# A second level of Strassen's algorithm for one of the seven gate and up products, and the down weights' sums moved to VectorE

## The chip, the cores and the metric

The kernel runs on one core of one Trainium2 chip. The metric is the device time of one execution in microseconds (us), the median over the runs shown; the profile is one further execution, recorded instruction by instruction.

## The reference

One layer of a hybrid encoder on 2048 tokens of width 1024: a combined projection, forgetting attention beside a multi-scale pooling, attention to 256 memory tokens, and a gated feed-forward. Each part adds to the residual stream h. The change lies in the last part:

```python
D_FF = 2816
hn = rmsnorm(h, g_ffn[l])
gu = jnp.einsum('bsd,df->bsf', hn, w_gate_up[l])        # 2048 x 1024 times 1024 x 5632
act = jax.nn.silu(gu[..., :D_FF]) * gu[..., D_FF:]
h = h + jnp.einsum('bsf,fd->bsd', act, w_down[l])       # 2048 x 2816 times 2816 x 1024
```

All of it is fp32.

## The kernel before

**Words and products.** A matmul here takes fp32r operands, which keep only part of an fp32 number. So each operand is split in two words: ACT casts it to the high word, VectorE subtracts that from the original to get the low word (`sub_hi`, L64; the cast is on L1137 for gate and up weights, L184 for `split`). `mm3` (L66 to L71) forms a product of two such pairs with three matmuls: high times high (L69), high times low (L70), low times high (L71). With a contraction of 128 a chunk, a product over 512 of the width is 4 chunks, 12 matmuls.

**Feed-forward, gate and up** (`gate_up`, from L1518). The tokens are handled in two passes (`ps_`) of 1024. The 2816 features are 22 tiles `t` of 128. For one tile the weights are a 2 x 2 block matrix: two halves of the width of 1024 (512 each) by gate and up (128 features each), b11, b12, b21, b22; the pass's tokens are x11, x12, x21, x22: two groups of 512 tokens by the two halves of the width. One level of Strassen's algorithm (Winograd's form) makes the four results from seven products instead of eight: b11 with x11, b21 with x12, t4 with x22, b22 with s4, t2 with s2, t1 with s1, t3 with s3, where t1 to t4 are sums of weight blocks and s1 to s4 sums of token blocks. Each product is 12 matmuls of 512 columns, 84 a tile. `product` (L1513) issues one; `weight_steps` (L1130) makes the weights' words and sums (splits on L64, sums on L1140).

PSUM has eight banks of 512 fp32 columns. A tile uses a, b and c, banks 0 to 2 or 3 to 5 in turn. a collects b11, then t2, then t3 on top of each other, and after each step ACT copies the running sum to SBUF (s1 on L1534, s2 on L1566, s3 on L1572); t4 of this tile follows in the next tile's turn. b holds t1, later b22 on top. c holds b21 with x12, and VectorE adds it to s1 (L1551), after which ACT applies silu (L1552): that is the first token group's gate. The order on TensorE for tile t, with the tile before it interleaved, is: b11, t4 of t-1, b21, b22 of t-1, t2, t1, t3. Banks 6 and 7 are free for the late token tiles of the first pass.

**What is ready when.** The token operands' words of a pass are kept in SBUF: four of them in large slabs (`SLABS`: x11, x12, s2, s1; they appear in the trace under the slabs' old names qs, kh, kl, cb) and three made at the start of the stage (`late_ops`: s3, x22, s4) from raw tiles `xr`, loaded from DRAM. Weight words go to eight places ww0 to ww7 in turn (`word_pair`), seven parts a tile. The raw weights of a tile (`graw`, 1 MB) have two buffers. `temp` (L1438) hands out [128, 512] fp32 tiles from a pool of 14: the copies s1, s2, s3, the activations and their sums, raw operands.

**Side jobs in the first pass** are hung on places in the tile loop (`early`, L1670 on): (t, n) is a place in tile t. From tile 4 on, the last four token tiles are normalised and turned (`late_tile`; PE transposes to banks 6 and 7, VectorE multiplies them into `hst`). For each pair of tiles, `load_down` brings a 1 MB group of down weights (`wdr`), and `down_sums` (L1482) makes their four Strassen sums on POOL (L1486) and stores them to DRAM for the down product, which both passes read. POOL also makes the activations' sums (`act_sums`, L1510).

**Feed-forward, down** (`down`): per pass seven products over 11 pairs of feature tiles, each step with one split of activations and one of weights; in the first pass's down, the second pass's token operands are made in between (`next_ops`).

**Order of the work.** In this stage TensorE and SP (the queue that issues the loads) run in the order in which the code is written (`in_order(EN.SP)`). For ACT, VectorE and POOL a planner fixes the order beforehand from modelled costs and due times; each engine then works through its queue in that order, and waits where an input is missing. A tile of a pool is taken by whichever instruction is next in the planner's time when one is free.

Of the kernel before, what the change touches and what calls it, by code (L numbers as in the profile page):

```python
# [16 lines left out]
P = 128  # L17
S = 2048
D = 1024
KD = D // P  # L20
# [21 lines left out]
def block_kernel(ctx: ExitStack, tc: tile.TileContext, x, xT, memT, cols, rows, w_qkvf, w_p, w_pool, w_out,  # L42
# [1013 lines left out]
    SLABS = ("x11", "x12", "s2", "s1")  # L1056
# [6 lines left out]
    late_d = {op: [dr.tile([P, FT], F32, name=f"{op}d{j}") for j in range(4)] for op in ("s3", "s4")}  # L1063
# [66 lines left out]
    def weight_steps(raw, w, tie=()):  # L1130
        b = {(kh, a): raw[:, 4 * kh:4 * kh + 4, a] for kh in range(2) for a in range(2)}
        quad = lambda v: v.rearrange("p (k c) -> p k c", k=4)
        sum_ = lambda n: quad(hp.tile([P, FT], F32, tag="cm", name=n, bufs=3)[:])

        def put(nm, v):
            w[nm] = hi, lo = word_pair()
            needs(act.copy(quad(hi), v), *(tie if nm == "t2" else ()))  # L1137
            sub_hi(quad(lo), v, quad(hi))

        sub = lambda o, p_, q_: dve.tensor_tensor(out=o, in0=p_, in1=q_, op=ALU.subtract)  # L1140
# [12 lines left out]
        put("t3", b[0, 1])  # L1153
        sub(b[1, 0], b[1, 0], t2)
        put("t4", b[1, 0])
        put("b22", b[1, 1])
        yield

    def weight_ops(raw, tie=()):
        w = {}  # L1160
        for _ in weight_steps(raw, w, tie):
            pass
        return w
# [270 lines left out]
    with hps, ExitStack() as c0:  # L1434
# [3 lines left out]
        temp = lambda n: fb.tile([P, FT], F32, tag="t", name=n, bufs=14)[:]  # L1438
        bank = lambda n: fps.tile([P, FT], F32, tag=f"bk{n}", name=f"bk{n}", bufs=1)[:]
        OPS = ("x11", "x12", "s2", "s1", "s3", "s4", "x22")  # L1440

        def late_ops():

            for op in ("s4", "s3", "x22"):
                ops[op] = [tuple(fb.tile([P, FT], F32R, tag=f"{op}{c}{j}", name=f"{op}{c}{j}", bufs=1)[:]
                                 for c in "hl") for j in range(4)]

        def load_late(op):

            late_raw[op] = [temp("xr") for _ in range(4)]  # L1450
            for j in range(4):
                sp.dma_start(late_raw[op][j], hTd[1][j + 4] if op == "x22" else late_d[op][j][:])
# [3 lines left out]
        def put_late(op):  # L1456
            for j in range(4):
                hi, lo = ops[op][j]
                needs(act.copy(hi, late_raw[op][j]), *(emptied[:1] if op in ("x22", "s3") else ()))
                sub_hi(lo, late_raw[op][j], hi)  # L1460

        late_raw = {}

        def late_tile(i):
# [3 lines left out]
            for a, hv in enumerate(halves):  # L1468
                sp.dma_start(hv, h2d[i][:, a * FT:(a + 1) * FT])
                act.activation(bank(6 + a), hv, AF.Square, scale=1.0 / 32.0, accum_out=ms[:, a:a + 1])  # L1470
# [5 lines left out]
            def turn_(a):  # L1476
                turn_normed(i, 4 * a, halves[a], bank(6 + a).rearrange("p (k t) -> p k t", k=4),
                            fb.tile([P, 4, P], F32, tag="hst", name="hst", bufs=1))
# [3 lines left out]
        def down_sums(k):  # L1482

            raw = down_raw.pop(k)
            b11, b12, b21, b22 = (raw[:, n] for n in range(4))
            sub = lambda o, p_, q_: pool.tensor_tensor(out=o, in0=p_, in1=q_, op=ALU.subtract)  # L1486
# [5 lines left out]
            for nm, v in (("t3", t3), ("t1", b12), ("t2", b22), ("t4", b21)):  # L1492
                pool.dma_start(wsum[k][nm][:], v)
# [3 lines left out]
        def load_down(k):  # L1497
            down_raw[k] = raw = wdp.tile([P, 4, FT], F32, tag="wd", name="wdr", bufs=1)
            for c in range(2):
                sp.dma_start(raw[:, 2 * c:2 * c + 2],  # L1500
                             w_down[:, (2 * k + c) * P:(2 * k + c + 1) * P, :].rearrange("a p c -> p a c"))
# [15 lines left out]

        def gate_up(ps_, between, follow, head, turned=0):  # L1518

            prev = None  # L1520
            blocks = {}
            for t in range(NF + 1):
                cur = None
                if t < NF:
                    for job in between.get((t, 0), ()):
                        job()
                    w = head if t == 0 and head else weight_ops(weights_raw(t, hp, "v"), copied[4:5] if t == 5 else ())
                    for job in between.get((t, 1), ()):
                        job()
# [3 lines left out]
                    s1 = temp("s1")  # L1533
                    emptied.append(act.copy(s1, a))  # L1534
                    for job in between.get((t, 2), ()):
                        job()
                else:
                    next(follow)
                if prev:
                    k, odd = divmod(prev["t"], 2)  # L1540
# [4 lines left out]
                    blocks["a22" if odd else "a21"] = prev["s3"]  # L1545
                    pool.dma_start(actd[prev["t"]][2 * ps_ + 1][:], prev["s3"])
                    if odd:
                        act_sums(ps_, k, blocks, ("s1", "s2"))
                if cur:
                    product(c, w["b21"], "x12", True)  # L1550
                    dve.tensor_tensor(out=s1, in0=c, in1=s1, op=ALU.add)  # L1551
                    act.activation(s1, s1, AF.Silu)  # L1552
                    cur["s1"] = s1
                else:
                    next(follow)
                if prev:
                    product(prev["b"], prev["w"]["b22"], "s4", False)
                    dve.tensor_tensor(out=prev["s2"], in0=prev["b"], in1=prev["s2"], op=ALU.add)
                    dve.tensor_tensor(out=prev["s2"], in0=prev["s2"], in1=prev["s1"], op=ALU.mult)
                    blocks["a12" if odd else "a11"] = prev["s2"]  # L1560
                    pool.dma_start(actd[prev["t"]][2 * ps_][:], prev["s2"])
                    act_sums(ps_, k, blocks, ("s4",) if odd else ("s3",))
                if cur:
                    product(a, w["t2"], "s2", False)
                    cur["s2"] = temp("s2")
                    copied.append(act.copy(cur["s2"], a))  # L1566
                    for job in between.get((t, 3), ()):
                        job()
                    product(b, w["t1"], "s1", True)
# [95 lines left out]
        with in_order(EN.SP):  # L1665
            for op in ("s3", "x22", "s4"):
                load_late(op)
            late_ops()
            turns = {}
            early = {(0, 2): [lambda: put_late("s3")], (0, 3): [lambda: put_late("x22")], (1, 1): [lambda: put_late("s4")]}  # L1670
# [4 lines left out]
            early.setdefault((0, 1), []).append(lambda: load_down(0))  # L1675
            for k in range(NK - 1):
                if k:
                    early.setdefault((2 * k + 2, 1), []).append(lambda k=k: load_down(k))
# [10 lines left out]

            for ps_ in range(2):  # L1690
# [53 lines left out]
```

## Time and profile before

| | us |
|---|---|
| median of 3 runs | 2486.38 (2486.14 to 2488.24) |
| the profiled execution | 2486.17 |
| its span, first to last instruction | 2484.4 |
| gate and up, first pass | about 1220 to 1637 of the span |
| down, first pass | about 1637 to 1848 |
| gate and up, second pass | about 1848 to 2268 |
| down, second pass | about 2268 to the end |

The granted TensorE clock was 0.999 of full speed on average. PE is TensorE's matmuls, PEld its weight loads, DVE is VectorE, ACT ScalarE, POOL GpSimd. A row of a group reads: line, engine, operation, tiles out<-in, shapes, count | busy us, mean ns of one | idle time of the engine just before, and what ended it. A row of a timeline reads: start, length, engine, line, operation.

### The profile page before, as it was taken

Reading aid. Unit: us, or ns where it says so; the run is one execution under the profiler, and the core shown is the slowest. Engines: PE = TensorE matmul, PEld = TensorE weight load, DVE = VectorE, ACT = ScalarE, POOL = GpSimd, SP = SyncE. Lnnn points to the kernel's source line nnn. Section 1 sums busy time; section 2 is a strip of 40 time slices with the busy share of each in tenths; the row PEclk is TensorE's granted clock in tenths of the full one; section 3 lists DMA queues with packets and bytes.
Section 4 is the critical chain, followed back from the end, with each engine's and each line's share of the span. In section 5 each row is a group of like instructions: output and inputs, shape, how many; then the busy total and the mean of one; then the engine's idle time right before and its main releaser. Section 6 shows DMA issues by size and latency. Waiting matters only on the chain.

```text
span 2484.4 us, 36567 instructions
## 1 busy us (share of the span) xinstructions
PE 2468.4 (99%) x12899; PEld 2109.2 (85%) x12899; DVE 1662.4 (67%) x3000; ACT 1204.0 (48%) x2308; POOL 745.1 (30%) x1012
## 2 busy tenths in 40 slices
PE   9999999999999899999999999999999999999999
PEld 8999989878888788888888888888888888888887
DVE  7444495489999855556868787667676666665554
ACT  6434341089999835445633433335443333333443
POOL 2223200045556524343135545430002222222000
PEclk9999999999999999999999999999999999999999
DMA  8665566476776443233645544467762333325666
GB/s 295 216 191 173 163 210 180 150 197 159 177 166 156 120 149 112 106 111 134 233 158 182 193 174 167 172 230 251 259 239 98 106 119 115 107 98 198 229 204 212
DMA packets 218279, 428.95 MB, mean 173 GB/s; under 512 B 25952, under 2 KB 101728, under 8 KB 207264
## 3 DMA queue, kind: packets, MB, share of 16 engines
q1 hardware_dynamic: 187920, 330.12, 42.4%
q0 software_dynamic: 30032, 96.23, 10.4%
q8 instruction: 102, 1.67, 0.3%
q14 instruction: 81, 0.66, 0.1%
q10 hardware_dynamic: 144, 0.26, 0.0%
HBM read 287.47 MB, written 134.61 MB: 170 GB/s over the span
## 4 chain that ended last, share of the span: by engine, by line
PE 83%; DVE 1%; issue 1%; POOL 1%; ACT 0%; DVEq 0%; POOLq 0%; ACTq 0%
PE bk L71 17%; PE bk L69 17%; PE bk L70 17%; PE acc L917 5%; PE sps L841 5%; PE tp L56 4%; PE mmps L69 4%; PE mmps L71 4%; PE mmps L70 4%; PE oo L69 1%; PE oo L70 1%; PE oo L71 1%; PE zp L71 1%; PE zp L69 1%; PE zp L70 1%
## 5 line engine op out<-in xcount | busy, mean ns | idle before, releaser
L64 DVE TENSOR_TENSOR ww<-draw,ww 128x512 fp32r<-128x512 f32 x308 | 209.7, 719 | 151.1 <-ACT ww L184 150.6
L184 ACT CAST ww<-draw 128x512 fp32r<-128x512 f32 x308 | 179.2, 620 | 220.9 <-PE bk L71 175.3
L64 DVE TENSOR_TENSOR ww<-graw,ww 128x512 fp32r<-128x512 f32 x220 | 174.3, 798 | 107.8 <-ACT ww L1137 107.6
L70 PE MATMUL bk<-ww,ww 128*128 128x512 f32 x619 | 240.2, 388 | 0.0
L71 PE MATMUL bk<-ww,ww 128*128 128x512 f32 x619 | 240.2, 388 | 0.0
L69 PE MATMUL bk<-ww,ww 128*128 128x512 f32 x619 | 240.1, 388 | 0.0
L1137 ACT CAST ww<-graw 128x512 fp32r<-128x512 f32 x220 | 136.0, 622 | 179.5 <-PE bk L71 164.4
L64 DVE TENSOR_TENSOR pl<-tp,ph 128x512 fp32r<-128x512 f32 (+3 forms) x298 | 177.5, 598 | 7.3 <-ACT ph L950 6.6
L69 PE MATMUL zps<-wh,xhi 128*128 128x384 f32 (+1 forms) x512 | 174.1, 340 | 0.0
L71 PE MATMUL zps<-wh,xl 128*128 128x384 f32 (+1 forms) x512 | 172.0, 336 | 0.0
L70 PE MATMUL zps<-wl,xhi 128*128 128x384 f32 (+1 forms) x512 | 171.9, 336 | 0.0
L950 ACT CAST ph<-tp 128x512 fp32r<-128x512 f32 (+3 forms) x298 | 152.7, 529 | 24.3 <-PE tp L56 22.9
L69 PE MATMUL bk<-qs,ww 128*128 128x512 f32 x352 | 137.8, 391 | 0.0
L71 PE MATMUL bk<-qs,ww 128*128 128x512 f32 x352 | 137.2, 390 | 0.1
L70 PE MATMUL bk<-kh,ww 128*128 128x512 f32 x352 | 136.9, 389 | 0.0
L69 PE MATMUL bk<-kl,ww 128*128 128x512 f32 x352 | 136.9, 389 | 0.0
L70 PE MATMUL bk<-cb,ww 128*128 128x512 f32 x352 | 136.9, 389 | 0.0
L71 PE MATMUL bk<-kl,ww 128*128 128x512 f32 x352 | 136.9, 389 | 0.0
L71 PEld LDWEIGHTS bk<-ww,ww 128*128 128x128 f32 x619 | 116.2, 188 | 24.1
L70 PEld LDWEIGHTS bk<-ww,ww 128*128 128x128 f32 x619 | 116.2, 188 | 24.0
L69 PEld LDWEIGHTS bk<-ww,ww 128*128 128x128 f32 x619 | 116.2, 188 | 23.7
L1615 POOL DMA_DIRECT2D out_dram<-o x31 | 16.7, 541 | 374.9 <-DVE o L1612 373.0
(641 smaller groups left out, 7066.1 us busy)
## 6 DMA issues: line engine op xcount, KB each, us to landing
graw<-in_w_gu_dram SPq DMA_DIRECT2D x44, 1024.0 KB, 5.6
draw<-in_w_down_dram SPq DMA_DIRECT2D x66, 256.0 KB, 4.4
xl<-in_xT_dram SPq DMA_DIRECT2D x64, 256.0 KB, 5.5
wdr<-in_w_down_dram SPq DMA_DIRECT2D x22, 512.0 KB, 4.3
xrow<-in_x_dram SPq DMA_DIRECT2D x16, 512.0 KB, 4.8
vd<-cb SPq DMA_DIRECT2D x16, 512.0 KB, 3.6
kh<-qkT1h SPq DMA_DIRECT2D x16, 512.0 KB, 10.3
kl<-qkT1l SPq DMA_DIRECT2D x16, 512.0 KB, 12.3
```

The lines of the kernel that those rows point to most:

```text
L56: return pe.transpose(out.bitcast(F32R), src, identr[:])
L64: (eng or dve).tensor_tensor(out=lo, in0=src, in1=f(hi), op=ALU.subtract)
L69: pe.matmul(ps, lhsT=sh, rhs=mh, start=first, stop=False, skip_group_check=goes_on)
L70: pe.matmul(ps, lhsT=sh, rhs=ml, start=False, stop=False, skip_group_check=goes_on)
L71: pe.matmul(ps, lhsT=sl, rhs=mh, start=False, stop=last, skip_group_check=goes_on)
L184: act.copy(hi, raw)
L841: pe.matmul(ps[:, :w], lhsT=qs[:, i * P:(i + 1) * P], rhs=kk[:, cs], start=(a == 0), stop=(a == 1))
L917: pe.matmul(acc[:m, q0 * P:], lhsT=v[:, j, :m], rhs=(pl if low else ph)[:, q0 * P:], start=state["n"] == 1, stop=state["n"] == 2 * nk)
L950: act.copy(ph[:, sl], tp[:, sl])
L1137: needs(act.copy(quad(hi), v), *(tie if nm == "t2" else ()))
L1615: pool.dma_start(out[rows_, cs], o)
```

## The change

**Weights and products.** The product b21 with x12, two of which belong to a pair of feature tiles (even t, odd t+1), is made for the pair at once: the two tiles' b21 side by side are 512 of the width by 256 features, x12 is 512 of the width by 512 tokens. Both are cut in 2 x 2 blocks (256 of the width by 128 features; 256 of the width by 256 tokens), and the same form of Strassen's algorithm gives seven quarter products, each of 2 chunks, that is 6 matmuls of 256 columns. The odd tile's turn issues all seven, between the other products; the order there is b11, three quarters, t4 of t-1, two quarters, b22 of t-1, two quarters, t2, t1, t3. In even tiles the order is b11, t4 of t-1, b22 of t-1, t2, t1, t3. In tile 0, where there is no tile before, t1 comes ahead of t2: b11, t1, t2, t3. The quarters gather in halves of bank 7 (u) and of the c banks, and VectorE adds them to s1 of both tiles in six sums of 256 columns and one of 512; both silus follow at the end of the odd tile's quarters.

```diff
@@ weight_steps
         put("b11", b[0, 0])
-        put("b21", b[1, 0])
...
+        if pair is None:
+            t4 = b[1, 0]
+            sub(t4, b[1, 0], t2)
+        else:
+            t4 = b[0, 0]
+            sub(t4, b[1, 0], t2)
+            odd = b[1, 0]
+            put_half(pair, "h11", "h21")
+            both = sum_("ht")
+            sub(both[:, :2], odd[:, :2], pair[:, :2])
+            sub(both[:, 2:], odd[:, 2:], both[:, :2])
+            put_half(both, "ht1", "ht2")
+            sub(odd[:, :2], odd[:, 2:], odd[:, :2])
+            put_half(odd, "ht3", "h22")
+            sub(pair[:, 2:], pair[:, 2:], both[:, 2:])
+            put_half(pair[:, 2:], "ht4")
@@ gate_up
+                        if odd:
+                            pair = fb.tile([P, 4, P], F32, tag="pair", name="pair", bufs=1)[:]
+                            sp.dma_start(pair, w_gu[t - 1].rearrange("p (k a c) -> p k a c", k=KD, a=2)[:, 4:, 0])
...
+                if odd:
+                    u, c0, c1 = bank(7)[:, :B], bank(3 * ((t + 1 + turned) % 2) + 2), c[:, B:]
+                    s0 = prev["s1"]
+                    quarter(u, w["h11"], "a11", True)
+                    quarter(c1, w["ht1"], "s1", True)
+                    quarter(c0[:, :B], w["h21"], "a12", True)
+                    add(s0[:, :B], u)
+                    add(s1[:, B:], c1)
...
-                if cur:
-                    product(c, w["b21"], "x12", True)
-                    dve.tensor_tensor(out=s1, in0=c, in1=s1, op=ALU.add)
-                    act.activation(s1, s1, AF.Silu)
...
+                if odd:
+                    quarter(u, w["ht2"], "s2", False)
+                    quarter(c1, w["h22"], "s4", False)
+                    add(s1[:, :B], u)
+                    add(s1[:, :B], c1)
...
+                if odd:
+                    quarter(u, w["ht3"], "s3", False)
+                    quarter(c0[:, B:], w["ht4"], "a22", True)
+                    add(s0[:, B:], u)
+                    add(s1[:, B:], u)
+                    add(s0, c0)
+                    for s_ in (s0, s1):
+                        act.activation(s_, s_, AF.Silu)
...
                 if cur:
+                    if not prev:
+                        product(b, w["t1"], "s1", True)
                     product(a, w["t2"], "s2", False)
...
+                    if prev:
+                        product(b, w["t1"], "s1", True)
                     product(a, w["t3"], "s3", False)
```

An odd tile needs the even tile's b21 once more, as a separate load `pair` of 256 KB.

**Token operands.** x12 leaves the slabs and s3 takes its place. x12's quarter operands (its four blocks, and sums s1 to s4 of them) are made by a new function, at the start of the first pass from raw tiles (after the first product's bank has been copied), and for the second pass late in the first pass's down.

```diff
+        def quarter_ops(raws, *after):
...
+            for j in range(2):
+                r0, r1 = raws[j], raws[j + 2]
+                put(first_, j, r0[:, :B])
+                put(wide[0], j, r1)
+                tt(r1[:, B:], r0[:, B:], r1[:, B:], ALU.add)
+                tt(r0[:, B:], r0[:, :B], r0[:, B:], ALU.subtract)
+                tt(r0[:, :B], r1[:, B:], r0[:, :B], ALU.subtract)
+                tt(r1[:, :B], r1[:, :B], r0[:, :B], ALU.subtract)
+                put(wide[1], j, r1)
+                put(wide[2], j, r0)
+        def quarter(ps, wop, xop, first):
+            for j in range(2):
+                cs = slice(j * P, (j + 1) * P)
+                mm3(ps, (wop[0][:, cs], wop[1][:, cs]), quarters[xop][j], first and j == 0, j == 1, not first)
...
-            for op in ("s3", "x22", "s4"):
+            for op in ("x12", "x22"):
                 load_late(op)
...
+            def last_op():
+                load_late("s4")
+                put_late("s4")
...
-            early = {(0, 2): [lambda: put_late("s3")], (0, 3): [lambda: put_late("x22")], (1, 1): [lambda: put_late("s4")]}
+            early = {(0, 2): [lambda: quarter_ops(late_raw["x12"], *emptied[:1])], (0, 3): [lambda: put_late("x22")],
+                     (1, 1): [last_op]}
...
+                between[68] = [next_quarters]
```

**Down weights and buffers.** The down sums go from POOL to VectorE, in place; the down weights are loaded as four tiles of 256 KB into `temp`, which now has 12 tiles and also holds `hst`. The late tiles' transposes use bank 6 alone.

```diff
-        temp = lambda n: fb.tile([P, FT], F32, tag="t", name=n, bufs=14)[:]
+        temp = lambda n: fb.tile([P, FT], F32, tag="t", name=n, bufs=12)[:]
@@ down_sums
-            raw = down_raw.pop(k)
-            b11, b12, b21, b22 = (raw[:, n] for n in range(4))
-            sub = lambda o, p_, q_: pool.tensor_tensor(out=o, in0=p_, in1=q_, op=ALU.subtract)
-            t3 = temp("t3")
-            sub(t3, b22, b12)
-            sub(b12, b12, b11)
-            sub(b22, b22, b12)
+            b11, b12, b21, b22 = down_raw.pop(k)
+            sub = lambda o, p_, q_: dve.tensor_tensor(out=o, in0=p_, in1=q_, op=ALU.subtract)
+            sub(b11, b12, b11)
+            sub(b12, b22, b12)
+            sub(b22, b22, b11)
             sub(b21, b21, b22)
@@ load_down
+            down_raw[k] = [temp("wdr") for _ in range(4)]
+            for n, t_ in enumerate(down_raw[k]):
+                sp.dma_start(t_, w_down[n % 2, (2 * k + n // 2) * P:(2 * k + n // 2 + 1) * P, :])
```

More of the change, by code (lines that the diff above doesn't have):

```diff
@@ L1061, in block_kernel @@
                for p_ in range(2)]
-    late_d = {op: [dr.tile([P, FT], F32, name=f"{op}d{j}") for j in range(4)] for op in ("s3", "s4")}
+    late_d = {"s4": [dr.tile([P, FT], F32, name=f"s4d{j}") for j in range(4)]}
     ops = {}
@@ L1153, in weight_steps, with weight_ops @@
         put("t3", b[0, 1])
-        sub(b[1, 0], b[1, 0], t2)
-        put("t4", b[1, 0])
+        put("t4", t4)
         put("b22", b[1, 1])
         yield
-    def weight_ops(raw, tie=()):
+    def weight_ops(raw, tie=(), pair=None):
         w = {}
-        for _ in weight_steps(raw, w, tie):
+        for _ in weight_steps(raw, w, tie, pair):
             pass
@@ L1688, in next_ops, with next_quarters @@
                     pass
+            def next_quarters():
+                raws = [temp("xr") for _ in range(4)]
+                for j in range(4):
+                    sp.dma_start(raws[j], hTd[2][j + 4])
+                quarter_ops(raws)
             for ps_ in range(2):
```

87 lines of the change are left out of this document (51 added, 36 removed).

## The prediction

> **What bounds the kernel now.** I read the page first: engine shares and the chain that ended last.
>
> ```profile
> span 2484.4 us, 36567 instructions
> PE 2468.4 (99%) x12899; PEld 2109.2 (85%) x12899; DVE 1662.4 (67%) x3000; ACT 1204.0 (48%) x2308; POOL 745.1 (30%) x1012
> PE 83%; DVE 1%; issue 1%; POOL 1%; ACT 0%; DVEq 0%; POOLq 0%; ACTq 0%
> ```
>
> TensorE holds the chain, but a busy TensorE may still hide small waits, so the next view is the busy time by stretches of the feed-forward (start and end, length, then PE, PEld, DVE, ACT and POOL busy, clock, DMA share, GB/s). The first row is the start of the first pass, the second tiles 4 to 11 of it, the third a pair of late tiles, the fourth a pair of tiles in the second pass.
>
> ```profile
> 1226.00:1246.00 20.00, 19.91 (x89) 16.15 (x88) 19.84 (x34) 14.05 (x25) 0.55 (x1) 1.00 0.49 181
> 1296.00:1448.00 152.00, 152.00 (x688) 125.81 (x687) 121.55 (x132) 61.62 (x115) 78.55 (x98) 1.00 0.53 184
> 1562.00:1600.00 38.00, 38.00 (x169) 31.47 (x168) 27.74 (x32) 13.80 (x25) 17.17 (x20) 1.00 0.45 166
> 1962.00:2000.00 38.00, 38.00 (x169) 31.48 (x168) 24.33 (x32) 13.79 (x25) 9.62 (x12) 1.00 0.32 111
> ```
>
> In steady state TensorE never stops and VectorE has a quarter to a third of its time free. Only in the first 26 us is VectorE full (19.84 of 20.00), and there lies the one wait of TensorE: a weight load held by a VectorE split (timeline: start, length, engine, line).
>
> ```profile
> 1225.72 0.69 DVE L1551 TENSOR_TENSOR s<-bk,s 128x512 f32<-128x512 f32 x1 [3.64 <-PE bk L71]
> 1226.92 2.49 DVE L64 TENSOR_TENSOR s3l<-xr,s3h 128x512 fp32r<-128x512 f32 x4
> 1229.33 2.49 DVE L64 TENSOR_TENSOR x22l<-xr,x22h 128x512 fp32r<-128x512 f32 x4
> 1233.54 1.29 DVE L64 TENSOR_TENSOR ww<-graw,ww 128x512 fp32r<-128x512 f32 x2
> 1234.28 0.19 PEld L71 LDWEIGHTS bk<-qs,ww 128*128 128x128 f32 x1 [0.52 <-DVE ww L64]
> ```
>
> So the price of a product is its matmuls, start to start; a matmul's own printed length (0.39 us at 512 columns) overlaps the next. From the timeline, first and last of three unbroken runs: 31 matmuls of 512 columns in the feed-forward, 24 of 256 columns in the memory attention (weights from a ww tile, as the new quarter products have), 18 of 256 columns at the very end.
>
> ```profile
> 2268.00 0.39 PE L69 MATMUL bk<-ww,ww 128*128 128x512 f32 x1
> ...
> 2274.80 0.39 PE L69 MATMUL bk<-s4h,ww 128*128 128x512 f32 x1
> ```
> ```profile
> 1205.34 0.28 PE L69 MATMUL mops<-pTh,ww 128*128 128x256 f32 x1
> ...
> 1208.05 0.28 PE L71 MATMUL mops<-pTh,ww 128*128 128x256 f32 x1
> ```
> ```profile
> 2478.80 0.28 PE L69 MATMUL bk<-ww,ww 128*128 128x256 f32 x1
> ...
> 2480.83 0.28 PE L71 MATMUL bk<-ww,ww 128*128 128x256 f32 x1
> ```
>
> That is 6.80/30 = 226.7 ns, 2.71/23 = 117.8 ns and 2.03/17 = 119.4 ns.
>
> **The change, part by part.** *Matmuls.* For each of 11 pairs of feature tiles in each of 2 passes, 24 matmuls of 512 columns (two b21 products) become 42 of 256 (seven quarter products of 2 chunks and 3 word products). 24 x 226.7 = 5.44 us; 42 x 117.8 = 4.95 us: 0.49 us a pair, 22 pairs, **-10.8 us**. With 119.4 ns it is -9.4 us. I take 117.8: its weights and its moving operand lie as in the quarters. The halving of the columns alone would give 3 of 24 matmuls, 15 us; the 4 ns by which 117.8 exceeds half of 226.7 eat the rest. The Trainium skill ("TensorE: Matmul & The Clock Gate", section "Back-to-back issue gap") gives columns/2.4 GHz + 2.5 ns, so 109 and 216 ns; by it the gain would be 13.0 us. Both widths run slower than that in this trace, so the rows decide.
>
> *Tile 0 of each pass.* With no tile before it, t1 now goes ahead of t2, so that t3 follows t2 at once into a bank that ACT must first copy. How long such a handover takes:
>
> ```profile
> 1963.82 0.39 PE L71 MATMUL bk<-qs,ww 128*128 128x512 f32 x1
> 1964.24 0.59 ACT L1534 COPY s<-bk 128x512 f32<-128x512 f32 x1 [1.57 <-PE bk L71]
> ```
>
> 0.42 us from the last matmul's start to the copy, 0.59 us of copy, about 0.05 us back (the first of the two splits from 1233.54 ends 0.69 us later, at 1234.23, and the load it releases starts at 1234.28), less the 0.23 us that the next matmul would have waited anyway: 0.8 us, twice, **+1.7 us**. Before, t1's 2.7 us of matmuls covered it. If ACT is busy with the operands' casts just then, one cast of 0.6 us more; bounds 1 to 4 us.
>
> *The start of the first pass.* x12's 28 quarter parts are made after the first product's bank copy, from about 1224. A 512-wide VectorE operation starts 0.60 us after the one before (2.49 us for four); a 256-wide one costs about 0.35, its printed length being
>
> ```profile
> L64 DVE TENSOR_TENSOR pl<-tp,ph 128x256 fp32r<-128x256 f32 x32 | 13.4, 418 | 0.3 <-ACT ph L950 0.3
> ```
>
> 6 splits of 512, 2 of 256 and 8 sums of 256 make 7.1 us, against 2.4 us for the four s3 splits that go; tile 1's extra weight parts (below) add some 3 us and its bank sums 1.5 us. Against that the 3.64 us of idle at 1225.7 shrink, and TensorE, without b21, comes to tile 1 2.7 us sooner. Taking the operands in the order in which they fall due, with tile 1's first quarter at 1234.5, the operands up to ht1 are ready 2.8 us early, x22's about 1 us, h22 just then (16.0 us of VectorE work by 1240), s4 at 1241 to 1243 for a use from 1240.8 to 1242.8. s4 is now loaded only when x12's raw tiles come free, and its loads take
>
> ```profile
> xr<-s4d SPq DMA_DIRECT2D x4, 256.0 KB, 7.1
> ```
>
> 7.1 us. A work list that fits only in the best order costs something: I take **+2 us**, bounds 0 (the old 0.5 us wait can go as well) and 7 us (s4 a whole landing late, or VectorE's extra work uncovered).
>
> *Steady state, VectorE.* A pair loses two b21 splits, gains 3.5 splits for h and ht parts, four 256-wide sums, and six 256-wide and one 512-wide bank sums for two 512-wide: 1.5 x 0.69 + 4 x 0.42 + 6 x 0.42 - 0.69 = 4.5 us. In the first pass the four down sums move here: 4 x 0.69 = 2.8 us. But POOL's sums stretch VectorE now. Groups by line, first in the stretch 1296 to 1448, then in 2000 to 2190 (no POOL down sums):
>
> ```profile
> L1140 DVE TENSOR_TENSOR t<-graw 128x512 f32<-128x512 f32 x8 | 16.4, 2044 | 0.0
> ```
> ```profile
> L1140 DVE TENSOR_TENSOR t<-graw 128x512 f32<-128x512 f32 x10 | 6.8, 684 | 0.1
> ```
>
> 2044 against 684 ns for the same subtraction. The pair rows above give the whole toll: 27.74 - 24.33 = 3.4 us. So a late first-pass pair needs 27.7 - 3.4 + 2.8 + 4.5 = 31.6 us of VectorE, a pair of tiles 4 to 11 30.4 + 3.9 = 34.3 us, a second-pass pair 28.8 us, of 37.6 us (14 products of 12 matmuls before, 38.1, less 0.49). The Trainium skill ("SBUF — State Buffer", section "Who interferes with whom") says that a VectorE operation with two SBUF inputs and a GpSimd operation that reads SBUF exclude each other whole; the 2044 ns row agrees. Without that give-back the busiest pairs would stand at 37.7 us, over TensorE's time. VectorE hides all this as long as its order fits the due times: **+1 us**, bounds 0 and the rival below.
>
> *Steady state, banks.* In even tiles b22 now comes 5.4 us after t3 (b11, t4) instead of 8.2. It waits for the copy and the sum of that bank:
>
> ```profile
> 1980.14 0.39 PE L71 MATMUL bk<-s3h,ww 128*128 128x512 f32 x1
> 1980.56 0.59 ACT L1572 COPY s<-bk 128x512 f32<-128x512 f32 x1 [2.04 <-PE bk L71]
> 1981.18 0.69 DVE L1573 TENSOR_TENSOR s<-bk,s 128x512 f32<-128x512 f32 x1 [1.94 <-ACT s L1572]
> ```
>
> done 1.7 us after the last matmul's start: 3.7 us to spare. The quarter banks are read twice; between two uses lie a whole product and two quarters (2.7 + 1.4 us), against 0.2 to 0.4 us of wait and two 0.42 us sums. The eight places for weight parts now take 16 parts a pair instead of 14; counted through, the shortest way from a place freed to its part's use is 6.9 us (t3 of odd tiles), against some 1.5 us for cast and split. These cost nothing unless VectorE's queue is some 3 us late.
>
> *Queues and buffers.* SP gets a 256 KB pair load per odd tile and 256 KB down loads instead of 512 KB ones. The down loads now wait for shared temporaries (12, formerly 14), and the next tile's weights are queued behind them on SP. Those weights land in
>
> ```profile
> graw<-in_w_gu_dram SPq DMA_DIRECT2D x15, 1024.0 KB, 7.4
> ```
>
> 7.4 us, but their own buffer frees some 19 us before use, so the down loads may wait about 10 us unnoticed. That ACT copies do wait for a temporary is visible already, without cost to TensorE:
>
> ```profile
> ACT s L1534 <- POOL wdr L1486: 9.4, 5, 2.1
> ```
>
> Taken at nothing; it is in the rivals' bounds. The memory stage swaps four x12 splits for four s3 splits and drops four small stores: nothing.
>
> **Sum.** -10.8 + 1.7 + 2 + 1 = -6.1 us. The profiled execution took 2486.17 us (span 2484.4 and 1.8 around it) and would take 2480.1; the median of the runs is 2486.38, so 2480.3 us. What a measurement of this kernel can tell from no change is about 0.2%, 5.0 us: faster is below 2481.4, slower above 2491.4.
>
> **The rivals.** *1. The start and the temporaries eat the gain.* For it: 19.84 of 20.00 us at the start, and 9.4 us of ACT waits on temporaries with 14. Against it: the due-time count above closes. With 7 us at the start, 4 at the two tiles 0 and 1 in steady state, the time is 2486.4 - 10.8 + 12 = 2487.6; with half of what that adds to the forecast, 2484. Chance 0.20, no measurable change.
>
> *2. VectorE becomes the bound in the first pass.* Place: tiles 4 to 13, where late tiles' turns share the stage. It needs 34.3 us of 37.6, but in that stretch it also idles for its inputs (7.6 us a pair by the 121.55 of 152.00), and an in-order queue cannot fill all of it. If half of that idle stays, a pair takes 34.3 + 3.8 = 38.1; with the down loads' landing misjudged by the planner, so that a down sum stands at the head of VectorE's queue, 2 to 3 us more, 40.5. That is 3 us for each of 5 pairs, 15 us: 2480.3 + 15 = 2495 us. It decides from 2.2 us a pair (11 us, which takes it past 2491.4). Against it: TensorE had no wait at 80% VectorE load. Chance 0.15.
>
> *3. Each narrow matmul costs a fixed amount.* The pair breaks even at 5.44/42 = 129.5 ns. The load of the weights is printed as 0.19 us (row at 1234.28); if loads could not overlap, 42 x 0.19 = 8.0 us, 2.5 us a pair lost, 55 us: 2542. Against it: 24 loads in 2.71 us above. Chance 0.03. The same section of the Trainium skill also gives streams of load and matmul as 81 ns at 128 and 131 ns at 512 columns; an estimate between them, 98 ns, would make the change lose 21 us. The 226.7 ns at 512 contradict it here.
>
> *4. No stall but the tiles 0.* 2486.4 - 10.8 + 1.2 = 2476.8 us. For it: TensorE's record in steady state. Chance 0.12.
>
> **How the numbers follow.** Forecast 0.50, its stalls 2 to 8 us, so 2478 to 2483: two thirds of it below 2481.4 (0.34), the rest within (0.16). Faster 0.34 + 0.12 = 0.46; same 0.16 + 0.20 = 0.36; slower 0.15 + 0.03 = 0.18. The range goes from case 4 to the near edge of case 2, 2476 to 2492, and leaves out most of cases 2 and 3 (0.17) and little else.
>
> **What would show it.** Right: 924 matmuls of 256 columns in the quarters, start to start 117 to 120 ns; a gap of about 0.8 us ahead of t3 in tile 0 of both passes; waits of 1 to 3 us in tile 1 of the first pass; no others above 0.3 us; a steady pair 37.6 us long; no 2 us VectorE sums caused by POOL down sums; VectorE 30 to 35 us a pair in the first pass. Wrong: narrow matmuls at 125 ns or more; TensorE waits that return each pair, behind VectorE (case 2) or behind copies that wait for a temporary; weights that land late behind the down loads.

## The result, and the profile after

The changed kernel took 2595.96 us (median of 4 runs, 2588.45 to 2601.45), the kernel before 2486.9 us on the same chip: 1.0436 times as long, 95% interval 1.0409 to 1.0463. The forecast was 2480.3 us. The profiled execution has these shares and this chain:

```profile
span 2593.3 us, 37970 instructions
...
PE 2496.7 (96%) x13295; PEld 2138.0 (82%) x13295; DVE 1743.8 (67%) x3310; ACT 1228.3 (47%) x2360; POOL 682.3 (26%) x964
...
PE 71%; DMA 5%; DVE 4%; issue 3%; POOL 2%; ACT 2%; SPq 0%; POOLq 0%; ACTq 0%; DVEq 0%
```

TensorE fell from 99% to 96% busy, and DMA, which was not on the chain at all, has 5% of it. VectorE's share is the same 67%, so the first look does not point to a full VectorE, though an average over the whole span settles little. Busy time by stretches says where. The three stretches are first gate and up, first down, second gate and up, cut at the first matmul of each pass and behind the last product of its last tile; the columns are as in the prediction. The kernel before:

```profile
1219.98:1648.52 428.54, 428.45 (x1905) 354.40 (x1904) 316.17 (x373) 171.35 (x307) 188.58 (x228) 1.00 0.49 175
1648.52:1852.52 204.00, 204.00 (x901) 168.92 (x900) 146.22 (x223) 100.44 (x176) 19.16 (x29) 1.00 0.77 263
1852.52:2276.84 424.32, 424.32 (x1873) 351.35 (x1872) 265.61 (x356) 156.39 (x272) 103.40 (x130) 1.00 0.32 111
```

The changed kernel:

```profile
1222.35:1742.89 520.54, 453.83 (x2103) 374.28 (x2101) 332.67 (x539) 180.76 (x326) 134.61 (x189) 0.95 0.41 146
1742.89:1964.09 221.20, 210.17 (x901) 172.81 (x901) 152.52 (x246) 105.80 (x186) 13.60 (x24) 0.97 0.75 257
1964.09:2385.69 421.60, 420.88 (x2071) 357.11 (x2070) 325.72 (x477) 165.48 (x294) 103.19 (x129) 1.00 0.32 118
```

The first pass is 92.0 us longer, the first down product 17.2 us, the second pass 2.7 us shorter; the second down product takes 204.0 us in both, and the stage before ends 2.4 us later. Together 108.9 us, the difference of the spans. So the products themselves gain (second pass), and the loss lies where the down weights are loaded. The waits of TensorE, and then of SP's queue, from 1260 to 1740 (waiting engine, line and tile, what it waited for: us in all, times, longest):

```profile
PE bk L69 <- ACT ww L1137: 45.5, 10, 6.6
PE bk L69 <- ACT ww L1145: 11.6, 10, 1.8
PE bk L71 <- DVE ww L64: 3.2, 10, 0.7
```
```profile
SPq L1549 <- POOL s L1558: 103.3, 20, 19.7
SPq L1549 <- DVE s L1612: 42.8, 7, 6.8
SPq L1520 <- DMA wt2k<-wdr: 39.1, 3, 13.3
SPq L1549 <- DMA hTd<-hst: 36.7, 2, 24.7
```

Ten waits, one a pair: TensorE waits for ACT's cast of b11 (L1137). L1549 is the load of down weights; it waits for a temporary that POOL's activation sums (L1558), VectorE (L1612) or the store of a turned late tile (`hst`, which is a temporary now) still hold. L1520 is the load of a late token tile; it waits for a temporary whose down sum is still being stored. One pair (tiles 12 and 13) in the timelines of SP, ACT and TensorE:

```profile
1507.66 7.82 SPq L1549 DMA_DIRECT2D wdr<-in_w_down_dram  x4
1515.57 0.38 SPq L1127 DMA_DIRECT2D graw<-in_w_gu_dram  x1
1516.00 0.43 SPq L1588 DMA_DIRECT2D pair<-in_w_gu_dram  x1
```
```profile
1524.02 0.62 ACT L1137 CAST ww<-graw 128x512 fp32r<-128x512 f32 x1 [3.03 <-DMA graw<-in_w_gu_dram]
```
```profile
1519.93 0.39 PE L71 MATMUL bk<-kl,ww 128*128 128x512 f32 x1
1524.69 0.80 PE L69 MATMUL bk<-qs,ww 128*128 128x512 f32 x1 [4.37 <-ACT ww L1137]
1525.28 0.63 PE L70 MATMUL bk<-kh,ww 128*128 128x512 f32 x1
1525.71 0.63 PE L71 MATMUL bk<-qs,ww 128*128 128x512 f32 x1
1526.13 0.63 PE L69 MATMUL bk<-qs,ww 128*128 128x512 f32 x1
```

The four down loads hold the head of SP's queue until 1515.5: the first of them waits for the store of `hst` until 1507.6, the last for a sum of POOL until 1515.1. The odd tile's weights, next in the queue, go out at 1515.57, land at about 1524.0, are cast, and b11 starts at 1524.69, 4.5 us late. Then the matmuls start 0.43 us apart instead of 0.227, and the granted clock from 1524.7 to 1530 is 0.51: the wait is followed by half rate for some microseconds. In the whole first pass 44 gaps of over 0.46 us make 72.6 us beyond 0.227 us each, and 90 matmuls at half rate 17.6 us more. The kernel before has one such gap, of 0.5 us, and no half rate, although its down load (L1500) waits at the head of SP's queue as well, for its own tile's stores:

```profile
SPq L1500 <- DMA wt4k<-wdr: 104.1, 10, 18.5
```

Such a wait costs nothing as long as it ends early; what changed is what it waits for.

### The profile page after: what moved, and what is told of

The parts are those of the page before. It is cut to its first block, busy times and chain, and to the rows that moved or that the text cites. A ratio compares the mean times of both kernels' runs of the same rounds, so it can differ in the third digit from the quotient of the medians.

```text
span 2593.3 us, 37970 instructions
## 1 busy us (share of the span) xinstructions
PE 2496.7 (96%) x13295; PEld 2138.0 (82%) x13295; DVE 1743.8 (67%) x3310; ACT 1228.3 (47%) x2360; POOL 682.3 (26%) x964
## 4 chain that ended last, share of the span: by engine, by line
PE 71%; DMA 5%; DVE 4%; issue 3%; POOL 2%; ACT 2%; SPq 0%; POOLq 0%; ACTq 0%; DVEq 0%
PE bk L71 14%; PE bk L69 14%; PE bk L70 14%; PE sps L841 4%; PE acc L917 4%; PE tp L56 4%; PE mmps L69 3%; PE mmps L71 3%; PE mmps L70 3%; DMA graw<-in_w_gu_dram 2%; DMA pair<-in_w_gu_dram 2%; PE oo L70 1%; PE oo L69 1%; PE oo L71 1%; POOL s L1558 1%
## 5 line engine op out<-in xcount | busy, mean ns | idle before, releaser
L64 DVE TENSOR_TENSOR ww<-draw,ww 128x512 fp32r<-128x512 f32 x308 | 204.2, 703 | 147.1 <-ACT ww L184 146.8
L1137 ACT CAST ww<-graw 128x512 fp32r<-128x512 f32 x176 | 108.8, 620 | 217.8 <-PE bk L71 168.8
L69 PE MATMUL bk<-qs,ww 128*128 128x512 f32 x352 | 146.6, 417 | 45.5 <-ACT ww L1137 45.5
L64 DVE TENSOR_TENSOR ww<-graw,ww 128x512 fp32r<-128x512 f32 x198 | 166.0, 840 | 26.2 <-ACT ww L1137 25.2
L71 PE MATMUL bk<-qs,ww 128*128 128x512 f32 x352 | 143.8, 409 | 1.5 <-DVE ww L64 1.5
L70 PE MATMUL bk<-kh,ww 128*128 128x512 f32 x352 | 144.1, 409 | 0.0
L71 PEld LDWEIGHTS bk<-ww,ww 128*128 128x128 f32 x619 | 117.5, 190 | 24.1
L841 PE MATMUL sps<-kh,qs 128*128 128x512 f32 (+2 forms) x320 | 124.5, 389 | 0.8 <-DVE mx L843 0.4
```

The source lines that it names most:

```text
L64: (eng or dve).tensor_tensor(out=lo, in0=src, in1=f(hi), op=ALU.subtract)
L69: pe.matmul(ps, lhsT=sh, rhs=mh, start=first, stop=False, skip_group_check=goes_on)
L70: pe.matmul(ps, lhsT=sh, rhs=ml, start=False, stop=False, skip_group_check=goes_on)
L71: pe.matmul(ps, lhsT=sl, rhs=mh, start=False, stop=last, skip_group_check=goes_on)
L841: pe.matmul(ps[:, :w], lhsT=qs[:, i * P:(i + 1) * P], rhs=kk[:, cs], start=(a == 0), stop=(a == 1))
```

## The experiments

Theory A: loads and operations at the head of in-order queues (SP's above all) wait for buffers, and what TensorE needs next stands behind them. Theory B: VectorE, which has the down sums now, is too late. Each time is a median, beside the kernel before on the same chip (2486.6 to 2487.0 us).

**Order alone** (`e1_weights_first`). The down loads go behind the odd tile's weights instead of ahead of them (in the kernel before they stood at place 1 of the even tile, the change has them at place 3; both are ahead of the odd tile's weights):

```diff
-early.setdefault((2 * k + 2, 3), []).append(lambda k=k: load_down(k))
-early.setdefault((2 * k + 3, 1), []).append(lambda k=k: down_sums(k))
+early.setdefault((2 * k + 3, 1), []).append(lambda k=k: load_down(k))
+early.setdefault((2 * k + 3, 3), []).append(lambda k=k: down_sums(k))
```

> The changed kernel, with the four down loads of a pair issued on SP after the odd tile's weights instead of before them, and the VectorE sums half a tile later. Theory A (the down loads wait for a shared temporary at the head of SP's queue, and the odd tile's weights stand behind them): the 4 to 6 us of TensorE idle ahead of every odd tile's b11 goes, and with it the half clock after it; first-pass gate and up falls from 520 us to 425 to 440 us and the time to 2495 to 2515 us (the 17 us lost in the first down mostly stay). Theory B (the down sums stand at the head of VectorE's queue and wait for their loads): the loads now come even closer to the sums, so the stalls stay, 2570 to 2620 us.

**Engine alone** (`e2_pool_sums`): the sums in `down_sums` on `pool.tensor_tensor`, all else as changed.

> The changed kernel with the four down sums of a pair back on POOL, in place, and everything else as changed: the loads stay in the temporaries and ahead of the odd tile's weights. Theory A: the temporaries are freed no sooner, the stalls ahead of b11 stay or grow, 2580 to 2640 us. Theory B: VectorE no longer waits for a down load, 2485 to 2510 us.

Measured: the order gave 2504.27 us (1.0072 [1.0057, 1.0087]), the engine 2601.55 us (1.0465 [1.0448, 1.0482]). The first two stretches with the order exchanged:

```profile
1222.10:1655.85 433.75, 427.38 (x2103) 361.19 (x2101) 349.05 (x539) 179.48 (x326) 135.73 (x189) 1.00 0.50 175
1655.85:1875.13 219.28, 209.18 (x902) 172.05 (x901) 152.55 (x246) 106.13 (x186) 13.60 (x24) 0.97 0.74 259
```

The same work in another order on SP (the sums follow half a tile later): the first pass falls from 520.54 to 433.75 us, by 86.8 us, with the granted clock back at 1.00. Theory B falls for these stalls, and `e2_pool_sums` says the same: with the sums back on POOL theory B expected 2485 to 2510 us. In the first down product VectorE does have a part (below, under the account of the prediction).

**Each half alone.** `e3_down_part_alone` puts the down half of the change on the kernel before (12 temporaries, four loads into them, sums on VectorE, `hst` among them); `e4_quarters_alone` takes the down loads and sums out of the changed kernel, and the down product reads plain blocks of the down weights where it read their sums.

> The kernel before, with only the second half of the change: 12 temporaries instead of 14, down weights loaded into them at the changed place, hst in them, sums on VectorE; no quarter products, b21 with x12 as before. Theory A: the stalls ahead of b11 belong to this half; the first pass loses 60 to 100 us against the kernel before, 2545 to 2590 us. If instead the quarter products make the stalls (their longer odd tile, their extra VectorE work), 2485 to 2500 us.

> The changed kernel without the down loads and down sums: the down product reads plain blocks of the down weights where the sums would be, so its result is another one; the loads and matmuls of the down product are as many as before. What is left of the change is the quarter products and the 12 temporaries. Both theories: no idle ahead of b11; the quarters' 120 ns a matmul give 9.3 us, less 1 to 2 us in the two tiles 0, 2 to 8 us at the start, 0 to 6 us in the first down and 2 us in the memory stage: 2480 to 2493 us. If the quarter products themselves cause stalls in the first pass, above 2510 us.

Measured: 2551.41 us (1.0261 [1.0244, 1.0277]) and 2502.7 us (1.0066 [1.0051, 1.0081]). The stalls come with the down half; but the quarters alone are no gain either, which I had not expected. The first two stretches of the quarters alone:

```profile
1219.56:1657.70 438.14, 428.42 (x2104) 361.02 (x2102) 338.27 (x506) 183.85 (x333) 113.57 (x149) 1.00 0.35 127
1657.70:1868.70 211.00, 207.06 (x901) 170.84 (x900) 145.15 (x236) 102.15 (x179) 11.54 (x20) 0.98 0.73 255
```

Against the kernel before that is 9.6 us more in the first pass (about 9 us lost in tiles 0 and 1, and four gaps of 1.2 us where late tiles are turned, less what the narrow matmuls gain), 7.0 us more in the first down, and 3.6 us more after the last matmul, which stays unexplained and came in no other kernel.

**Place or buffer** (`e9_own_buffer`): order as in `e3_down_part_alone`, but the loads have a tile of their own.

```diff
-            down_raw[k] = [temp("wdr") for _ in range(4)]
+            own = wdp.tile([P, 4, FT], F32, tag="wd", name="wdr", bufs=1)
+            down_raw[k] = [own[:, n] for n in range(4)]
```

> The kernel of e3_down_part_alone (the down half of the change put on the kernel before, 2551.4 us, no quarter products) with the four down weight tiles landing in a tile of their own, as they do in the kernel before, instead of four shared temporaries. Their place in SP's order, ahead of the next odd tile's weights, their size and the sums on VectorE are as in e3_down_part_alone. Theory A (the load at the head of SP's queue waits for a temporary, and the weights behind it with it): nothing is left to wait for, the first gate and up pass falls from 487 us to 428 to 433 us and the total to 2490 (2486 to 2496). Rival D (the place itself is the cost: four more loads share SP and the DMA engines just ahead of the weights): the first pass stays over 460 us and the total over 2525.

Measured: 2503.3 us (1.0064 [1.0047, 1.0080]). First pass without and with its own buffer:

```profile
1222.40:1707.34 484.94, 447.47 (x1905) 363.29 (x1903) 267.97 (x406) 168.22 (x300) 133.78 (x188) 0.96 0.42 151
```
```profile
1222.24:1665.64 443.40, 433.86 (x1906) 357.79 (x1904) 298.07 (x417) 172.82 (x307) 139.91 (x193) 0.99 0.48 172
```

41.5 us go with the wait for a temporary, the place in the queue unchanged, and no wait for b11's cast is left: in this kernel, which still has only 12 temporaries, the shared buffer was the cause of those waits, and rival D is out. But 14.9 us over the kernel before remain, where I expected at most 5. They are four gaps of 2.4 to 3.9 us ahead of t3, each behind ACT's copy of t2's bank. In the timelines of VectorE, POOL and TensorE for the second of them:

```profile
1346.84 3.95 DVE L1485 TENSOR_TENSOR wdr<-wdr 128x512 f32<-128x512 f32 x2
1350.71 0.68 DVE L1140 TENSOR_TENSOR t<-graw 128x512 f32<-128x512 f32 x1
```
```profile
1346.57 1.30 POOL L1508 TENSOR_TENSOR s<-s,s 128x512 f32<-128x512 f32 x1
...
1348.93 1.30 POOL L1508 TENSOR_TENSOR s<-s,s 128x512 f32<-128x512 f32 x1
```
```profile
1353.18 0.39 PE L71 MATMUL bk<-kl,ww 128*128 128x512 f32 x1
1355.59 0.77 PE L69 MATMUL bk<-s3h,ww 128*128 128x512 f32 x1 [2.02 <-ACT s L1564]
```

Two down sums take 3.95 us on VectorE beside POOL's activation sums; the weights' sums behind them are late, ACT's cast waits for these, and the bank's copy stands behind the cast. So it is for three of the four gaps, and this is the prediction's second rival in small. The first and longest gap, in tile 0, comes before any down sum: there the copy stands behind ACT's casts of s3, which start only at 1231.59; why they start so late stays open.

**The first down product** (`e5_first_down`) and **the start** (`e6_start_too`), each on top of the one before:

```diff
-                between = {20 + 14 * j: [lambda j=j: next_ops(j)] for j in range(4)}
-                between[68] = [next_quarters]
-                between.update({2: [lambda: load_down(NK - 1)], 5: [lambda: down_sums(NK - 1)]})
+                between = {16 + 12 * j: [lambda j=j: next_ops(j)] for j in range(4)}
+                between.update({57: [load_next], 60: [next_quarters], 65: [next_quarters], 70: [next_quarters]})
+                between.update({8: [lambda: load_down(NK - 1)], 11: [lambda: down_sums(NK - 1)]})
@@ e6_start_too
-            early = {(0, 2): [lambda: quarter_ops(late_raw["x12"], *emptied[:1])], ...
+            early = {(0, 2): [lambda: quarter_ops(late_raw["x12"])], ...
...
-                        product(b, w["t1"], "s1", True)
+                        product(b, w["t1"], "s1", True, (0, 1))
                     product(a, w["t2"], "s2", False)
...
-                    if prev:
-                        product(b, w["t1"], "s1", True)
+                    product(b, w["t1"], "s1", True, range(0 if prev else 2, 4))
```

> The kernel that loads the odd tile's weights ahead of the down weights (2504.3 us), with the first down product's share of the new work moved: the last four down loads and their sums go from steps 2 and 5 to steps 8 and 11, the second pass's operands from steps 20, 34, 48, 62 to 16, 28, 40, 52, and x12's quarter parts from one block at step 68 to two halves at steps 60 and 65, their raw tiles loaded at step 57. The work is the same. Theory A, that in-order queues (SP's and VectorE's) hold the down product's own loads and splits behind this work: the first down product falls from 219.3 us to 204 to 206, the total to 2489 (2486 to 2493). Rival C, that the added VectorE and DMA work itself is what the down product can't hide, wherever it stands: the first down product stays over 211 us and the total over 2496.

> The kernel of e5_first_down with two edits at the start of a pass: x12's quarter parts no longer wait for the first product's bank copy (the part that needs the tile of the first weights is made last), and in tile 0 the product t1 is cut in two, two chunks ahead of t2 and two between t2 and t3. Theory A (order, not amount): the VectorE idle time of about 3 us ahead of the quarter parts goes, and with it 3 to 6 us of the 8 us that TensorE waits in tiles 0 and 1; the 0.9 us gap ahead of t3 in tile 0 goes in the second pass. Total 4 to 7 us under e5_first_down: 2483 (2480 to 2487), so the change would be worth 0 to 6 us against the kernel before. Rival C (the start has more VectorE work than fits): within 2 us of e5_first_down.

> The kernel of e6_start_too with the down weights' sums back on GpSimd, all else the same. Theory A (the engine of these sums is not what decides): within 3 us of e6_start_too, VectorE's sums in the first pass stretched to 2 us again. Rival B (the sums' engine matters): over 5 us slower, since GpSimd's sums stretch VectorE in the pairs where late tiles are turned, or over 3 us faster.

Measured: 2493.5 us (1.0025 [1.0015, 1.0034]), 2487.68 us (1.0004 [0.9996, 1.0013]) and 2495.57 us (1.0034 [1.0022, 1.0047]). The first down product fell to 210.5 us, by 8.8 us where 13 to 15 were expected: one gap of 3.5 us behind the operands' steps stayed, and half rate after it. The start edits gave 5.8 us by the medians, as expected, though the time lies just above the expected 2480 to 2487. The two profiled executions are 8.3 us apart: 3.9 in the first pass (433.80 to 429.92), 1.0 in the second, where the gap ahead of t3 is gone, and 3.7 in the first down product, whose planned order changed with them. And with the stalls gone, the sums' engine does matter: `e7_pool_again` is 7.9 us slower, where theory A had said within 3. The stretch of about tiles 4 to 11 with the sums on VectorE, then on POOL, and the weights' low words on VectorE in each:

```profile
1296.00:1448.00 152.00, 152.00 (x764) 129.06 (x763) 124.58 (x194) 66.90 (x127) 55.73 (x82) 1.00 0.54 191
```
```profile
1296.00:1448.00 152.00, 146.24 (x724) 121.98 (x723) 124.89 (x163) 63.30 (x120) 76.43 (x95) 1.00 0.52 180
```
```profile
L64 DVE TENSOR_TENSOR ww<-t,ww 128x512 fp32r<-128x512 f32 x16 | 10.9, 684 | 0.0
```
```profile
L64 DVE TENSOR_TENSOR ww<-t,ww 128x512 fp32r<-128x512 f32 x14 | 16.5, 1181 | 0.0
```

VectorE is equally busy (124.6 and 124.9 us) with 16 down sums more in the first case, and TensorE gets through more matmuls (764 against 724): what VectorE does itself it saves by not being stretched. TensorE's waits in `e7_pool_again` are for a sum of a quarter bank (L1581), with stretched splits ahead of it in VectorE's queue:

```profile
PE bk L69 <- DVE s L1581: 6.9, 10, 1.4
```
```profile
1357.51 2.44 DVE L64 TENSOR_TENSOR ww<-t,ww 128x512 fp32r<-128x512 f32 x1
1359.87 2.24 DVE L64 TENSOR_TENSOR ww<-graw,ww 128x512 fp32r<-128x512 f32 x1
1362.04 0.74 DVE L1581 TENSOR_TENSOR s<-bk,s 128x256 f32<-128x256 f32 x2
```

So the move to VectorE is worth about 8 us here, as long as nothing else stalls. Not all of it need be the stretching: `e4_quarters_alone`, without down sums on either engine, has its four gaps of 1.2 us at the same bank sum, and the planner orders VectorE's queue anew in each kernel. The runs do not separate the two.

**Operand steps in halves** (`e8_halves`): the second pass's operand steps cut in two, s3's word split ahead of the cut.

```diff
+        put("s3", x21)
         yield
...
-        put("s3", x21)
@@ between
+                between.update({20 + 12 * j: [next_rest] for j in range(4)})
```

> The kernel of e6_start_too with each of the second pass's four operand steps in the first down product cut in two, four down steps apart, and s3's word split moved ahead of that cut (so also earlier in the memory stage, where x12's split stood before the change). What e6_start_too still loses against an undisturbed course is 2.8 us in the first down product, 1.1 us in the stage before the feed-forward and about 4.6 us in tiles 0 and 1 of the first pass. Theory A (bursts at the head of VectorE's queue): the first down product falls from 206.8 to 204 to 205 us and the stage before by up to 1 us: 2484.5 (2483 to 2487), which is within 0.2% of the kernel before. Rival C (the amount of VectorE work): no change, 2487 to 2489.

Measured: 2485.35 us, 0.9993 [0.9984, 1.0002], the best version: no difference from the kernel before that can be measured. First pass and first down, and the start from 1212:

```profile
1221.75:1651.57 429.82, 425.73 (x2103) 360.24 (x2102) 355.90 (x546) 183.50 (x333) 135.43 (x189) 1.00 0.50 179
1651.57:1855.57 204.00, 204.00 (x901) 168.92 (x900) 147.43 (x240) 102.64 (x180) 13.80 (x24) 1.00 0.79 274
```
```profile
1212.00:1246.00 34.00, 30.10 (x140) 24.35 (x138) 32.13 (x61) 19.14 (x35) 3.17 (x5) 1.00 0.57 207
```

The first down is back at 204.00 us. At the start VectorE works 32.1 of 34 us and TensorE still waits: there the amount of work looks like the limit, though no run took any of it away. The stage before did not gain; it ended between 0.4 us earlier and 2.4 us later over all these kernels, with no order in it that I could find, and stays open.

## Why the prediction was wrong

- **The step that failed: "the down loads may wait about 10 us unnoticed", "Taken at nothing".** The mechanism had been named, its price was 86.8 us in the first pass (`e1_weights_first`), of 109 us lost. The step set the landing of the weights against their own buffer coming free "some 19 us before use". It did not follow the temporaries: those that the down loads need come free only when the activations of the pair before are multiplied and summed, late in the even tile's turn. The weights' own margin was not the fault: in `e1_weights_first` tile 13's leave 24.1 us before its b11 (1448.53 and 1472.59), more than the 19 us assumed. In the changed kernel they leave 4.6 us before b11 is due (1515.57 and 1520.16), and they need 9.1 us (8.4 us to land, then the cast): so the down loads held them for an estimated 19 to 20 us, not 10. The row that was quoted there, 9.4 us of ACT waits for temporaries, was read as harmless because ACT's waits cost nothing; a DMA waiting in front of other DMAs costs whatever stands behind it. The bounds of this term were left to the rivals, where the first allows 1 us for the whole steady state; the line "weights that land late behind the down loads" was in the list of signs only.
- **A term left out.** The first down product had none. The last down loads there (from step 2) wait for temporaries ahead of the down product's own loads on SP, their four sums stand on VectorE ahead of its splits, and so do x12's quarter parts (step 68) later: 17.2 us. The loads, the sums and the wait at the start of that stretch:

```profile
1720.38 18.95 SPq L1549 DMA_DIRECT2D wdr<-in_w_down_dram  x4
```
```profile
1744.42 4.29 DVE L1536 TENSOR_TENSOR wdr<-wdr 128x512 f32<-128x512 f32 x4
```
```profile
1749.98 0.79 PE L70 MATMUL bk<-ww,ww 128*128 128x512 f32 x1 [3.99 <-DVE ww L64]
```

  So the down sums' new engine costs some 4 us here, in the order that the change gave them; with the sums on POOL (`e2_pool_sums`) the first down product takes 217.6 us, 3.6 less. `e5_first_down`, `e6_start_too` and `e8_halves` gave it all back by moving work, none by leaving any out.
- **A cost of the stalls themselves.** The prediction had no price for what a wait does to the clock. After waits the matmuls ran 0.43 us apart and the granted clock of the first pass was 0.95: 17.6 us. The Trainium skill ("TensorE: Matmul & The Clock Gate", section "HAM oscillation — how this bites in real kernels") tells of the like: a wait for DMA in every round of a loop, after which TensorE starts at half rate each time. It speaks of waits over about 3.4 us; here 2.4 us could do it (below).
- **Matmuls, -10.8 us: too much.** A pair of tiles is 37.74 us long after the change, 38.08 before, in the second pass: 0.34 us a pair, 7.5 us in all, less than both prices of the prediction, 10.8 and 9.4. One run of quarters and the matmuls behind it show why:

```profile
2016.45 0.28 PE L69 MATMUL bk<-x12f,ww 128*128 128x256 f32 x1
...
2018.48 0.28 PE L71 MATMUL bk<-x12q,ww 128*128 128x256 f32 x1
2018.60 0.40 PE L69 MATMUL bk<-x22h,ww 128*128 128x512 f32 x1
2018.84 0.40 PE L70 MATMUL bk<-x22l,ww 128*128 128x512 f32 x1
```

  18 quarter matmuls are 2.03/17 = 119.4 ns apart, the end's 119.4 and not the memory attention's 117.8, which gives the 9.4 us; and after each run the first five 512-column matmuls start 0.229 to 0.236 us apart instead of 0.227, 0.08 us a pair, which was not thought of and takes the rest.
- **Tile 0, +1.7 us: nearly right.** The gap ahead of t3 was 0.9 us over the normal spacing in the second pass (forecast 0.8) and 1.7 in the first, where ACT was in its casts: 2.6 us, inside the bounds.
- **The start, +2 us: too little, at the upper end of its bounds of 0 to 7.** Besides tile 0, tile 1 waited 1.7 us for b11's low word, 0.9 and 0.6 us for ht1 and 2.4 us for a bank sum ahead of ht2, and eight matmuls ran at half rate, 1.6 us: about 7 us in all. The count of due times had tile 1's parts ready before their products; in the run VectorE took all of x12's and x22's parts first and came to b11's low word only at 1236.50, which was due at 1235.5.
- **Steady VectorE, banks, weight places: right.** With the queue's order mended the changed kernel has no wait over 0.25 us between tile 3 and the first pass's end, at 37.7 us a pair (38.7 where late tiles are turned), and in the second pass none but tile 0's.
- **The rivals.** None of them held the result. The second (VectorE) has its mechanism in the traces of `e9_own_buffer` and of the first down product, but of the 86.8 us nothing.

With the down loads behind the weights (`e1_weights_first`) the first gate and up pass is still 5.2 us longer than before and the second 2.7 us shorter: the forecast's own terms, as measured, make the kernel 2.5 us slower, and the first down product comes on top. So the change is no gain with its stalls mended, and `e8_halves` shows the same: 7.5 us won by the matmuls, about 5 us lost at the start of the first pass and 1.8 us in the stage before.

## What to carry to other kernels

When a load is moved onto shared buffers, cost it by when those buffers come free, and then by everything that stands behind it in its queue: the waits of an in-order queue are paid by its next customer. Before giving up a change whose steady state is sound, exchange the order of two loads: here one exchange of places took back 92 of 109 us. And a saving of 0.34 us a round, 22 rounds long, is gone at one start of 5 to 8 us, so count the places where the new operands are made before counting the rounds.

## What the runs showed of the hardware

Half rate came after shorter waits than I would have thought. In the changed kernel every gap of 2.4 us or more in gate and up was followed by 6 to 11 matmuls 0.35 to 0.46 us apart, and none of the gaps up to 2.07 us was. Near that border it is not regular: in `e9_own_buffer` two of three gaps of 2.4 us were followed by 6 or 7 such matmuls, one by none, and a gap of 2.48 us was followed by eight in the changed kernel and by none in `e2_pool_sums`. After that gap of the changed kernel the first twelve matmuls, 1.5 us of them, still ran at full rate. VectorE's 128x512 sums took 1.98 us instead of 0.69 us beside POOL's sums in `e9_own_buffer`; the Trainium skill ("SBUF — State Buffer", section "Who interferes with whom") tells of the two shutting each other out. Taking POOL's down sums out of its way was worth up to 7.9 us (`e7_pool_again` against `e6_start_too`).
